# The first loads of a one-core decoder step, dealt out anew to three DMA queues, with the lower bounds moved into the first chunk

## The chip, the cores and the metric

One Trainium2 chip, of which the program uses one core. The metric is the device time of one execution in microseconds (us); below, "a run" is one timed execution. Lower is better.

## The reference, cut to what matters

One inference step of a hybrid decoder layer (width 2048) for 256 prompt tokens and 8 sample tokens. Only the start of the layer matters here: a modulation vector worked out from the condition `c`, a normalised and modulated `x`, and the input projection of it.

```python
mod = jax.nn.silu(c) @ p['w_ada'][l] + p['b_ada'][l]
sh1, sc1, gt1, sh2, sc2, gt2 = jnp.split(mod[:, None, :], 6, axis=-1)
h = rmsnorm(x, p['g_pre_mix'][l]) * (1.0 + sc1) + sh1
z = h @ p['w_in'][l]
...
p = jax.nn.softmax(hg_lb.astype(jnp.float32), axis=0)
return jnp.maximum(jnp.cumsum(p, axis=0) - p[0:1], 0.0)
```

The last two lines are the lower bounds of one of three recurrent branches. They depend on one small input, `hg_lb` (1024 numbers), and are needed when that branch is worked out, after the first part of the input projection. After the mixer follow an output projection and a squared-ReLU MLP, all in float32 built from pairs of rounded halves.

## The kernel before, in words

**The work.** Every large product is done as three products of rounded halves: a weight block `raw` is loaded, ScalarE rounds it (`whi`, L667), VectorE takes what is left (`wlo`, L671), and TensorE multiplies `whi` and `wlo` with the halves of the activations (`mm`, issued through the helper at L89). The weights run through one long list of blocks (`Stream`, L629), in the order in which TensorE uses them.

**The start.** The input projection begins in "chunks" of K (`CHUNKS`, L36): chunk 0 multiplies the first two 128-wide slices of `h`, chunk 1 the next two, chunks 2 to 4 four each. So the first products need only two slices of `h`, hence only the 2 x 256 columns of `w_ada` that give shift and scale for these slices. Those are loaded by class `First` (L518): for chunk 0 there are 8 batches `b` of two DMAs each, every DMA 128 x 2 x 256 numbers (256 KB), 16 DMAs in all. One batch makes 8 products on TensorE (`ada`, through L89; the trace counts two for each).

What must happen ahead of the first `mm` product:

- `cst` (an identity matrix `ident` and ones, 128 KB) and the conditions `c_prompt` and `c_sample` are loaded, transposed by TensorE (L200, L201), and ScalarE takes their SiLU into `cT` (L204, L205), which every `ada` product uses.
- `b_ada`, `g_pre_mix` and `g_post_mix` go to the tile `st1` by ScalarE's queue (L189 to L191), eight small vectors to the tile `st2` by GpSimd's queue (L196). `small_vectors()` (L208) transposes both on TensorE (L93) and VectorE copies the result to `vec` (L212).
- The four quarters of `x` (512 KB each) are loaded by SyncE's queue (L186). ScalarE squares and sums each (L294); VectorE adds the sums (`ss`, L139), works out the reciprocal root in a chain of small instructions (L249 to L255) and leaves it in `rx` (L301); ScalarE and VectorE scale `x` by it (L317, L318); TensorE transposes the first four slices (L93, from L312).
- The 16 `ada` DMAs land, TensorE does the `ada` products: batches 0 to 3 ahead of the transposes of `x`, batches 4 to 7 behind them. Their sum is copied (`gt`, L349), transposed, and becomes shift and scale (`mod`, L139 from L554; `A1`, L560); then `modulate_first` (L489) makes the first halves of `h`.
- `lower_bounds()` (L224) runs in this stretch as well: an exponential (L228), a reciprocal, six small VectorE instructions, two logarithms (L235, L239) and two more.

**What sets the order.** TensorE's, SyncE's and GpSimd's instructions stand in the order of the program here; those of ScalarE and VectorE are placed by a scheduler until L869, and from L872 to L950 (the chunks) all five engines stand in program order. A DMA started from SyncE or ScalarE takes one of eight semaphores in turn (DMAHW0 to DMAHW7 in the listings), one from GpSimd takes one of eight others (DMASW0 to DMASW7): before a DMA is started, the one that had its semaphore must have landed. So of the SyncE and ScalarE DMAs together no more than eight are under way, and a DMA waits for the one eight places ahead of it in the program.

**The chunks.** In chunk 0 ten granules (index `gi`) of 24 products each follow each other. Between them ScalarE and VectorE round the next weights and copy each granule's two accumulators out (`evict`, L918 by ScalarE, L920 by VectorE); TensorE has two accumulators of each kind, so the next granule needs them free. Meanwhile GpSimd's queue loads the `ada` weights for chunk 1 (L532).

Of the kernel before, what the change touches and what calls it, by code (L numbers as in the profile page):

```python
# [10 lines left out]
AF = mybir.ActivationFunctionType  # L11
ALU = mybir.AluOpType
# [3 lines left out]
P = 128  # L16
D = 2048
KT = D // P
# [17 lines left out]
CHUNKS = (2, 2, 4, 4, 4)  # L36
# [33 lines left out]
def hybrid_step_kernel(  # L70
# [8 lines left out]
    nc = tc.nc  # L79
    V, S = nc.vector, nc.scalar  # L80
# [48 lines left out]
    def tmp(shape, tag, bufs=2):  # L129
        return tp.tile(shape, F32, tag=tag, name=nm(tag), bufs=bufs)  # L130

    def const(shape, name, dt=F32):
        return cp.tile(shape, dt, tag=name, name=name)

    def mul(o, a, b):
        V.tensor_tensor(o, a, b, op=ALU.mult)  # L136

    def add(o, a, b):
        V.tensor_tensor(o, a, b, op=ALU.add)  # L139

    def sub(o, a, b):
        V.tensor_tensor(o, a, b, op=ALU.subtract)  # L142
# [21 lines left out]


    cst = const([P, 904], "cst")
    nc.sync.dma_start(cst[:, 0:256], consts[:, 0:256])
# [5 lines left out]
    def flat128(v):  # L173
        return v.rearrange("l (k p) -> (l k) p", p=P)
# [3 lines left out]
    nc.scalar.dma_start(st_c[0:KT, :], c_prompt.rearrange("b (k p) -> (b k) p", p=P))  # L178
    nc.scalar.dma_start(st_s, c_sample.rearrange("b (k p) -> (b k) p", p=P))

    xt = [[blk([P, 1024]) for _ in range(2)] for _ in range(2)]
    xsr = blk([P, P])
    nc.sync.dma_start(xsr, x_sample.rearrange("b o (k p) -> (b o k) p", p=P))
    for t in range(2):
        for hf in range(2):
            nc.sync.dma_start(xt[t][hf], x_prompt[0, t * P:(t + 1) * P, hf * 1024:(hf + 1) * 1024])  # L186
# [4 lines left out]
    nc.scalar.dma_start(st1[112:128, :], flat128(g_post_mix))  # L191
    st2 = blk([P, P])
    rows2 = [(g_pre_mlp, 16), (g_post_mlp, 16), (hg_lb, 8), (gla_b_up, 4), (hg_norm_g, 1), (gla_norm_g, 2), (sgu_ln_g, 8), (sgu_ln_b, 8)]
    n2 = 0
    for v, n in rows2:
        nc.gpsimd.dma_start(st2[n2:n2 + n, :], flat128(v))  # L196
        n2 += n

    ps = sm()
    T.transpose(ps[:, 0:KT], st_c[0:KT, :], ident[0:KT, 0:KT])  # L200
# [21 lines left out]
    lnlb, lnom, dlt, oml = (const([P, 8], n) for n in ("lnlb", "lnom", "dlt", "oml"))  # L222

    def lower_bounds():  # L224

        lt = [tmp([P, 8], f"lb{i}", 1) for i in range(4)]
        sub(lt[0], lbrawT, lbrawT)
        S.activation(lt[0], lt[0], AF.Exp)  # L228
        V.reciprocal(lt[1], lt[0])
        mul(lt[0], lt[0], lt[1])  # L230
        sub(lt[1], lt[0], lt[0])
        V.tensor_scalar(lt[1], lt[1], 0.0, None, ALU.max)
        V.tensor_scalar(lt[2], lt[1], 0.0, -1.0e30, ALU.is_equal, ALU.mult)
        V.tensor_scalar(lt[3], lt[1], 1.0e-19, None, ALU.max)
        S.activation(lnlb, lt[3], AF.Ln)  # L235
        add(lnlb, lnlb, lt[2])
        V.tensor_scalar(oml, lt[1], -1.0, 1.0, ALU.mult, ALU.add)
        V.tensor_scalar(lt[3], oml, 1.0e-19, None, ALU.max)
        S.activation(lnom, lt[3], AF.Ln)  # L239
        sub(dlt, lnom, lnlb)  # L240


# [275 lines left out]
    class First:  # L518
# [5 lines left out]
            self.w, self.at = {}, {}  # L524

        def load(self, b):
            queue = nc.gpsimd if self.k0 else nc.sync
            w = blk([P, self.kn, 2, self.n * P])
            w1 = w_ada[0, :, 0:2 * D].rearrange("k (r c) -> k r c", r=2)
            for i in range(self.kn):  # L530
                k = b * self.kn + i
                queue.dma_start(w[:, i], w1[k * P:(k + 1) * P, :, self.k0 * P:(self.k0 + self.n) * P])  # L532
            self.w[b] = w.rearrange("p k r c -> p k (r c)")
            self.at[b] = step[0]

# [93 lines left out]
    class Stream:  # L629
# [167 lines left out]
    def new_acc():  # L797
        return pmm.tile([P, 2, 512], F32, tag="mm", name=nm("mm"))
# [55 lines left out]
    stream[0].half_at = gap_at[0]  # L854
    first = First(0, CHUNKS[0])
    for b in range(8):
        first.load(b)
    for i in (0, 1, 2):
        stream[0].load(i)
    small_vectors()  # L860
    lower_bounds()
    for b in range(4):
        first.steps(b)
    scale_rows(xt, rx)
# [29 lines left out]
    for ci, n in enumerate(CHUNKS):  # L894
# [2 lines left out]
            to_load += [(at, parts[-1], b) for b, at in enumerate(LOAD_AT[ci])]  # L897
        k0 += n
    k0 = 0
    for ci, n in enumerate(CHUNKS):  # L900
        final = ci == len(CHUNKS) - 1
        gn = 4 // n
        ng = len(begin) // gn
        if not final:
            nxt = parts[ci].paced()
        for gi in range(ng):
            if ci or gi:
                accs = [new_acc() for _ in range(gn)]
            todo = begin[gi * gn:gi * gn + gn]

            def evict(acc):

                c0, dst, fn = todo.pop(0)
                z = acc[:, :, 0:NT]
                if ci:
                    add(dst, dst, z)
                elif todo:
                    S.copy(dst, z)  # L918
                else:
                    V.tensor_copy(dst, z)  # L920
                if final and fn is not None:
                    S.activation(dst, dst, fn)

            def between():

                step[0] += 1
                if not final:
                    next(nxt, None)

            load_due()  # L930
            if ci or gi:
                granule(win, 0, n, begin[gi * gn][0], gn * CW, accs, hH, hL, k0, True, True, evict, between)
# [653 lines left out]
    for m in range(8):  # L1586
        if m in PRE_AT:
            n = N_PRE // len(PRE_AT)
# [341 lines left out]
```

## Time and profile before

| | |
|---|---|
| time, median of 3 runs (lowest to highest) | 1794.4 us (1793.9 to 1795.85) |
| span of the profiled execution, first to last instruction | 1792.8 us |
| TensorE busy with products | 1770.3 us (99%) |
| TensorE busy with weight loads | 1686.2 us (94%) |
| VectorE busy | 1183.8 us (66%) |
| ScalarE busy | 1002.5 us (56%) |
| GpSimd busy | 140.5 us (8%) |
| moved by DMA | 442 MB, mean 247 GB/s |
| granted TensorE clock | 1.00 |

The profile has no time of its own for the profiled execution but the span. The median of the runs is 1.6 us longer than that span.

How to read it: rows of the timeline give start and duration in us, the engine, the line of the kernel, the operation, "out<-in" by the names of the tiles (their numbers left out), the count, and in brackets the idle time ahead of it with what ended that. PE is TensorE, PEld its weight loads, DVE VectorE, ACT ScalarE, POOL GpSimd, SP SyncE; a "q" behind an engine is its own instruction queue, which starts DMAs. Rows of the DMA view give the queue, the count, the size of each and the median time from the start of the issue to landing.

### The profile page before, as it was taken

The numbers are of one execution on the slowest core, as the hardware profiler recorded it, in microseconds if no ns is written. First come the engines' busy times: TensorE is split into PE (matmuls) and PEld (weight loads), VectorE is DVE, ScalarE is ACT, GpSimd is POOL, SyncE is SP. The second block draws the span as 40 slices with busy tenths as digits, with TensorE's granted clock in tenths as the row PEclk, the third lists the DMA queues.
The fourth block names the chain that finished last, engine by engine and source line by source line (L and its number), as shares of the span: only waits on it lengthen the run. The fifth ranks groups of instructions, "written<-read, shape, count | busy, mean of one in ns | idle before, by whom it ended". The sixth has DMA issues, their size and how long they took to land.

```text
span 1792.8 us, 42113 instructions
## 1 busy us (share of the span) xinstructions
PE 1770.3 (99%) x16970; PEld 1686.2 (94%) x16970; DVE 1183.8 (66%) x2079; ACT 1002.5 (56%) x1823; POOL 140.5 (8%) x228
## 2 busy tenths in 40 slices
PE   6999999999999999999999999999999999999998
PEld 5899999989999999899999989999999999999997
DVE  5676668697588697466566666645666666666666
ACT  5444554666766766655455665555454545454544
POOL 4222000101102012110000010000000000000000
PEclk9999999999999999999999999999999999999999
DMA  9998597789699789898866946776666666666663
GB/s 343 392 354 296 184 340 249 227 293 309 208 290 320 236 285 311 286 370 264 266 193 206 319 140 220 239 254 204 193 196 198 194 197 195 194 199 192 198 191 117
DMA packets 330179, 442.05 MB, mean 247 GB/s; under 512 B 14946, under 2 KB 276944, under 8 KB 329984
## 3 DMA queue, kind: packets, MB, share of 16 engines
q1 hardware_dynamic: 312160, 381.05, 65.5%
q0 software_dynamic: 17184, 57.85, 9.2%
q8 instruction: 133, 2.18, 0.5%
q14 instruction: 62, 0.51, 0.1%
q10 hardware_dynamic: 640, 0.47, 0.1%
HBM read 427.60 MB, written 11.70 MB: 245 GB/s over the span
## 4 chain that ended last, share of the span: by engine, by line
PE 95%; DMA 2%; DVE 2%; ACT 1%; issue 0%; SPq 0%; DVEq 0%; ACTq 0%
PE mm L89 86%; PE ada L89 5%; PE sm L89 3%; PE sm L93 1%; DMA b<-in_w_ada_dram 1%; DVE wlo L671 1%; DMA b<-in_x_prompt_dram 0%; DVE b L139 0%; DVE b L1670 0%; DVE b L142 0%; ACT b L1356 0%; ACT b L145 0%; SPq L532 0%; SPq L186 0%; DVE b L136 0%
## 5 line engine op out<-in xcount | busy, mean ns | idle before, releaser
L89 PE MATMUL mm<-b,whi 128*128 128x264 f32 x9248 | 1578.8, 277 | 1.3 <-DVE b L920 0.4
L89 PEld LDWEIGHTS mm<-b,whi 128*128 128x128 f32 x9248 | 1394.4, 189 | 35.0 <-issue 19.9
L89 PE MATMUL mm<-b,wlo 128*128 128x264 f32 x4624 | 1275.5, 276 | 0.0
L671 DVE TENSOR_TENSOR wlo<-raw,whi 128x512 fp32r<-128x512 f32 x1118 | 760.3, 690 | 462.1 <-ACT whi L667 459.2
L667 ACT CAST whi<-raw 128x512 fp32r<-128x512 f32 x1118 | 681.7, 617 | 620.2 <-DVE wlo L671 315.6
L89 PEld LDWEIGHTS mm<-b,wlo 128*128 128x128 f32 x4624 | 873.5, 189 | 0.2
L139 DVE TENSOR_TENSOR b<-b,mm 128x528 f32<-128x528 f32 (+1 forms) x137 | 95.7, 699 | 55.6 <-PE mm L89 49.0
L89 PE MATMUL ada<-b,cT 128*32 128x256 f32 (+2 forms) x888 | 66.2, 421 | 3.4 <-DMA b<-in_w_ada_dram 3.1
L89 PEld LDWEIGHTS ada<-b,cT 128*32 128x32 f32 x888 | 26.1, 112 | 34.1 <-issue 17.2
L1860 POOL TENSOR_TENSOR gs<-b,G 128x16 f32<-128x16 f32 x1 | 0.2, 222 | 714.1 <-DVE b L139 714.1
L532 POOL DMA_DIRECT2D b<-in_w_ada_dram x64 | 46.3, 726 | 44.1 <-PE ada L89 35.1
L1214 POOL DMA_DIRECT2D out_dram<-st x32 | 23.5, 735 | 234.0 <-DVE st L1213 227.6
L667 ACT CAST whi<-araw 128x512 fp32r<-128x512 f32 x38 | 23.1, 618 | 26.2 <-PE mm L89 22.0
L89 PE MATMUL ada<-araw,cT 128*32 128x512 f32 x264 | 35.6, 599 | 0.0
L1211 ACT ACTIVATE st<-st,fs 128x128 f32<-128x128 f32 (+1 forms) x96 | 35.2, 426 | 0.0
L136 DVE TENSOR_TENSOR b<-b,b 128x512 f32<-128x512 f32 (+1 forms) x47 | 34.4, 747 | 1.2 <-ACT b L1325 0.8
L1213 DVE SCALAR_TENSOR_TENSOR st<-vbc,b,st 128x128 f32<-128x128 f32 (+1 forms) x96 | 32.4, 392 | 1.2 <-ACT st L1211 1.2
L93 PE MATMUL sm<-cst,b 128*128 128x128 f32 (+1 forms) x149 | 21.5, 285 | 8.2 <-DMA b<-in_g_post_mix_dram 5.0
L671 DVE TENSOR_TENSOR wlo<-araw,whi 128x512 fp32r<-128x512 f32 x38 | 24.6, 686 | 5.3 <-ACT whi L667 5.3
L93 PEld LDWEIGHTS sm<-cst,b 128*128 128x128 f32 (+1 forms) x149 | 17.5, 147 | 9.2 <-issue 6.0
L142 DVE TENSOR_TENSOR b<-b 128x1024 f32<-128x1024 f32 (+1 forms) x24 | 24.4, 1022 | 1.5 <-PE ada L89 1.4
L142 DVE TENSOR_TENSOR b<-gt,b 128x528 fp32r<-128x528 f32 x32 | 22.7, 709 | 3.6 <-ACT whi L667 0.5
(303 smaller groups left out, 819.5 us busy)
## 6 DMA issues: line engine op xcount, KB each, us to landing
raw<-in_w_in_dram SPq DMA_DIRECT2D x225, 512.0 KB, 5.2
raw<-in_w_mlp_down_dram SPq DMA_DIRECT2D x128, 512.0 KB, 3.6
raw<-in_w_mlp_up_dram SPq DMA_DIRECT2D x125, 512.0 KB, 3.9
araw<-in_w_ada_dram SPq DMA_DIRECT2D x66, 512.0 KB, 6.1
b<-in_w_ada_dram SPq DMA_DIRECT2D x62, 512.0 KB, 6.8
b<-in_w_ada_dram POOLq DMA_DIRECT2D x48, 512.0 KB, 9.6
raw<-in_w_branch_dram SPq DMA_DIRECT2D x48, 512.0 KB, 4.7
raw<-in_w_out_dram SPq DMA_DIRECT2D x32, 512.0 KB, 4.5
```

Of the source, the lines that this page charges most:

```text
L89: return nc.tensor.matmul(out, w, x, **kw)
L93: return nc.tensor.transpose(*a)
L136: V.tensor_tensor(o, a, b, op=ALU.mult)
L139: V.tensor_tensor(o, a, b, op=ALU.add)
L142: V.tensor_tensor(o, a, b, op=ALU.subtract)
L532: queue.dma_start(w[:, i], w1[k * P:(k + 1) * P, :, self.k0 * P:(self.k0 + self.n) * P])
L667: self.last = [S.copy(hi, raw).ins, None]
L671: self.last[1] = V.tensor_tensor(lo, raw, hi.bitcast(F32), op=ALU.subtract).ins
L1211: S.activation(st[:, i, :], st[:, i, :], AF.Copy, scale=fs[:, h0 + i, b:b + 1])
L1213: V.scalar_tensor_tensor(st[:, i, :], v[:, i, :], k[:, h0 + i, NP + b:NP + b + 1], st[:, i, :], ALU.mult, ALU.add)
L1214: nc.gpsimd.dma_start(G.s_out(b, h0, nh), st)
L1860: Q.tensor_tensor(gs[:, 14:16, :], dst[:, :, NP:NT], G2[:, 14:16, 1:NC], op=ALU.mult)
```

## The change

- `x` is the first thing that SyncE's queue loads. `cst` and `x_sample` ahead of it go to ScalarE's queue, behind `c_prompt` and `c_sample`.
- The 16 `ada` DMAs for chunk 0 are issued by a new helper, `load_first`: even batches by SyncE's queue (8 DMAs), odd batches by GpSimd's (8 DMAs, behind its eight small loads). Their tiles are taken earlier, and `First` only takes them over.
- `lower_bounds()` becomes a generator of four parts. It runs in chunk 0, one part each after granules 5, 6, 7 and 8: the exponential; eight VectorE instructions; the two logarithms together; the last two VectorE instructions. A third temporary is reused so that both logarithms can follow each other.

```diff
-    nc.sync.dma_start(cst[:, 0:256], consts[:, 0:256])
...
     nc.scalar.dma_start(st_c[0:KT, :], c_prompt.rearrange("b (k p) -> (b k) p", p=P))
     nc.scalar.dma_start(st_s, c_sample.rearrange("b (k p) -> (b k) p", p=P))
 
+    nc.scalar.dma_start(cst[:, 0:256], consts[:, 0:256])
     xt = [[blk([P, 1024]) for _ in range(2)] for _ in range(2)]
     xsr = blk([P, P])
-    nc.sync.dma_start(xsr, x_sample.rearrange("b o (k p) -> (b o k) p", p=P))
+    nc.scalar.dma_start(xsr, x_sample.rearrange("b o (k p) -> (b o k) p", p=P))
...
+    w_first = [blk([P, 2, 2, CHUNKS[0] * P]) for _ in range(KT // 2)]
+
+    def load_first(queue, b):
+
+        for i in range(2):
+            k = 2 * b + i
+            src = w_ada[0, k * P:(k + 1) * P, 0:2 * D].rearrange("p (r c) -> p r c", r=2)
+            queue.dma_start(w_first[b][:, i], src[:, :, 0:CHUNKS[0] * P])
+
+    at2 = 0
     for v, n in rows2:
-        nc.gpsimd.dma_start(st2[n2:n2 + n, :], flat128(v))
-        n2 += n
+        nc.gpsimd.dma_start(st2[at2:at2 + n, :], flat128(v))
+        at2 += n
+    for b in range(KT // 2):
+        load_first(nc.gpsimd if b % 2 else nc.sync, b)
...
         S.activation(lt[0], lt[0], AF.Exp)
+        yield
         V.reciprocal(lt[1], lt[0])
...
         V.tensor_scalar(lt[3], lt[1], 1.0e-19, None, ALU.max)
+        V.tensor_scalar(oml, lt[1], -1.0, 1.0, ALU.mult, ALU.add)
+        V.tensor_scalar(lt[0], oml, 1.0e-19, None, ALU.max)
+        yield
         S.activation(lnlb, lt[3], AF.Ln)
+        S.activation(lnom, lt[0], AF.Ln)
+        yield
         add(lnlb, lnlb, lt[2])
-        V.tensor_scalar(oml, lt[1], -1.0, 1.0, ALU.mult, ALU.add)
-        V.tensor_scalar(lt[3], oml, 1.0e-19, None, ALU.max)
-        S.activation(lnom, lt[3], AF.Ln)
         sub(dlt, lnom, lnlb)
...
     for b in range(8):
-        first.load(b)
+        first.w[b] = w_first[b].rearrange("p k r c -> p k (r c)")
...
     small_vectors()
-    lower_bounds()
...
+    bounds = lower_bounds()
...
             if ci == 0 and 2 * gi + 8 < KT:
                 x_transposed(2 * gi + 8)
+            elif ci == 0 and gi >= 5:
+                next(bounds, None)
```

Two places show how instructions move.

ScalarE, the first rows of the program before (`b_86`, `b_87` are the tiles of the conditions, `b_100` is `st1`, `sm_113` the transposed conditions):

```order
L178 DMA b_86<-in_c_prompt_dram 16x128
L179 DMA b_87<-in_c_sample_dram 128x128
L204 ACT_TABLE_LOAD [waits DVE_49]
L204 ACTIVATE cT<-sm_113 128x16 [waits PE_49]
L205 ACTIVATE cT<-sm_113 128x16x8
L189 DMA b_100<-in_b_ada_dram 96x128 [waits DMAHW0_49]
L190 DMA b_100<-in_g_pre_mix_dram 16x128 [waits DMAHW1_49]
L191 DMA b_100<-in_g_post_mix_dram 16x128 [waits DMAHW2_49]
```

The same place on ScalarE now (`b_94` is the tile of `x_sample`, `b_90` the first quarter of `x`, `sm_137` the transposed conditions):

```order
L177 DMA b_85<-in_c_prompt_dram 16x128
L178 DMA b_86<-in_c_sample_dram 128x128
L180 DMA cst<-in_consts_dram 128x256
L183 DMA b_94<-in_x_sample_dram 128x128
L216 ACT_TABLE_LOAD [waits DVE_49]
L216 ACTIVATE cT<-sm_137 128x16 [waits PE_49]
L217 ACTIVATE cT<-sm_137 128x16x8
L189 DMA b_100<-in_b_ada_dram 96x128 [waits DMAHW0_49]
L190 DMA b_100<-in_g_pre_mix_dram 16x128 [waits DMAHW1_49]
L191 DMA b_100<-in_g_post_mix_dram 16x128 [waits DMAHW2_49]
L309 ACTIVATE b_160,ss_22_158<-b_90 128x1024 [waits DMAHW4_49]
```

Two DMAs have come in ahead; the three loads of `st1` still stand behind the SiLU of the conditions, and the squares of `x` behind these.

VectorE, where the sums of squares meet the small vectors, before (`ss` the sums of squares, `vec` the transposed small vectors from `sm_211`, `rr` the reciprocal root):

```order
L303 COPY xx_127<-sm_147 128x8
L139 TENSOR_TENSOR ss_14_134<-ss_14_134 128x2 [waits Activation_49]
L212 COPY vec<-sm_211 128x191 [waits PE_49]
L249 TENSOR_SCALAR sx_150<-ss_14_134 128x2 [waits DVE_49]
L302 COPY xx_127<-ss_14_134 128x2
L213 TENSOR_SCALAR vec<-vec 128x3 [waits DVE_49]
L251 TENSOR_SCALAR rr_15_135<-sx_150 128x10 [waits DVE_49]
L142 TENSOR_TENSOR lb_43_216<-vec 128x8
```

The same place on VectorE now:

```order
L318 COPY xx_151<-sm_171 128x8
L224 COPY vec<-sm_211 128x191 [waits PE_49]
L225 TENSOR_SCALAR vec<-vec 128x3 [waits DVE_49]
L139 TENSOR_TENSOR ss_22_158<-ss_22_158 128x2 [waits Activation_49]
L264 TENSOR_SCALAR sx_174<-ss_22_158 128x2 [waits DVE_49]
L317 COPY xx_151<-ss_22_158 128x2
L266 TENSOR_SCALAR rr_23_159<-sx_174 128x10 [waits DVE_49]
L136 TENSOR_TENSOR sa_175<-rr_23_159 128x10 [waits DVE_49]
```

Both instructions on `vec` now stand ahead of the sum `ss`, and the first instruction of the lower bounds is gone from here.

More of the change, by code (lines that the diff above doesn't have):

```diff
@@ L193, in hybrid_step_kernel @@
     rows2 = [(g_pre_mlp, 16), (g_post_mlp, 16), (hg_lb, 8), (gla_b_up, 4), (hg_norm_g, 1), (gla_norm_g, 2), (sgu_ln_g, 8), (sgu_ln_b, 8)]
-    n2 = 0
+    n2 = sum(n for _, n in rows2)
+    w_first = [blk([P, 2, 2, CHUNKS[0] * P]) for _ in range(KT // 2)]
[5 more added lines that the diff above has]
+    at2 = 0
     for v, n in rows2:
-        nc.gpsimd.dma_start(st2[n2:n2 + n, :], flat128(v))
-        n2 += n
+        nc.gpsimd.dma_start(st2[at2:at2 + n, :], flat128(v))
+        at2 += n
+    for b in range(KT // 2):
+        load_first(nc.gpsimd if b % 2 else nc.sync, b)
     ps = sm()
@@ L526, in load @@
         def load(self, b):
-            queue = nc.gpsimd if self.k0 else nc.sync
             w = blk([P, self.kn, 2, self.n * P])
@@ L531, in load @@
                 k = b * self.kn + i
-                queue.dma_start(w[:, i], w1[k * P:(k + 1) * P, :, self.k0 * P:(self.k0 + self.n) * P])
+                nc.gpsimd.dma_start(w[:, i], w1[k * P:(k + 1) * P, :, self.k0 * P:(self.k0 + self.n) * P])
             self.w[b] = w.rearrange("p k r c -> p k (r c)")
```

## Prediction

> **What bounds the kernel now.** The page first: how busy each engine is, and the chain that ended last.
>
> ```profile
> span 1792.8 us, 42113 instructions
> PE 1770.3 (99%) x16970; PEld 1686.2 (94%) x16970; DVE 1183.8 (66%) x2079; ACT 1002.5 (56%) x1823; POOL 140.5 (8%) x228
> PE 95%; DMA 2%; DVE 2%; ACT 1%; issue 0%; SPq 0%; DVEq 0%; ACTq 0%
> ```
>
> TensorE bounds it: 99% busy, 95% of the chain. The 22.5 us in which it does nothing (1792.8 - 1770.3) are all this change can touch. Where they lie, the table of stages tells (stretch, its length, then busy us of PE, PEld, DVE, ACT, POOL, granted clock, DMA share, GB/s):
>
> ```profile
> 0.00:10.00 10.00, 1.54 (x5) 0.97 (x5) 2.06 (x9) 3.95 (x7) 5.54 (x15) 1.00 0.76 244
> 10.00:20.00 10.00, 6.93 (x71) 3.12 (x72) 4.93 (x29) 7.54 (x11) 0.00 (x0) 1.00 0.97 314
> 20.00:30.00 10.00, 8.05 (x103) 6.01 (x102) 4.68 (x13) 4.84 (x11) 2.86 (x5) 1.00 1.06 398
> 30.00:40.00 10.00, 9.26 (x81) 8.83 (x80) 8.86 (x15) 7.02 (x14) 8.04 (x12) 1.00 1.03 389
> 40.00:50.00 10.00, 10.00 (x138) 9.68 (x137) 5.41 (x10) 5.34 (x9) 4.33 (x6) 1.00 1.04 402
> ```
>
> TensorE idles 8.5, 3.1, 1.9 and 0.7 us in the first four stretches, 14.2 in all, then not at all from 40 to 50. From 40 us on it is fed, so a microsecond won or lost ahead of the first `mm` product is, as long as nothing behind it runs dry, one at the end. What holds up that first product, the chain in order of time and the timeline say:
>
> ```profile
> 3.06 8.79 DMA b<-in_x_prompt_dram
> 18.28 6.57 DMA b<-in_w_ada_dram
> ...
> 24.90 0.42 PE L89 MATMUL ada<-b,cT 128*32 128x128 f32 x8 [1.37 <-DMA b<-in_w_ada_dram]
> 27.25 0.72 PE L89 MATMUL mm<-b,whi 128*128 128x264 f32 x4
> ```
>
> The first two rows are of the chain, the others of the timeline. The last quarter of `x` lands at 3.06 + 8.79 = 11.85. The last `ada` DMA starts at 18.28, since it has to wait for the one eight places ahead of it, and lands at 24.85; the first `mm` product follows 2.4 later, at 27.25. A second path meets it, by way of the root of `x`:
>
> ```profile
> 11.94 1.06 ACT L294 ACTIVATE b<-b 128x1024 f32<-128x1024 f32 x1 [0.41 <-DMA b<-in_x_prompt_dram]
> 13.12 0.16 DVE L139 TENSOR_TENSOR ss<-ss 128x2 f32<-128x2 f32 x1 [6.52 <-ACT b L294]
> 13.20 0.35 DVE L212 COPY vec<-sm 128x191 f32<-128x191 f32 x1
> 15.91 2.19 ACT L317 ACTIVATE b<-b,rx 128x1024 f32<-128x1024 f32 x2 [1.30 <-DVE rx L301]
> 18.89 1.97 PE L93 MATMUL sm<-cst,b 128*128 128x128 f32 x8
> 51.76 1.95 PE L89 MATMUL ada<-b,cT 128*32 128x128 f32 x64
> ```
>
> From `ss` (13.12) it takes 2.8 to `rx` (L317 starts at 15.91), 1.1 for half of L317 (the first half of `x` is enough for these transposes), 1.97 for the transposes, 1.95 for four batches of `ada` products whose weights lie ready (the row from chunk 1), and 1.9 from the end of those to the first `mm` (24.90 + 0.42 to 27.25). Together 9.7 us from `ss`: alone, this path would have given the first product at 22.8. So today the weights decide, with 4.4 us in hand on the other path.
>
> **The change part by part.** Loads first, by these rows (those ahead of the dots are of the timeline, the others of the DMA view):
>
> ```profile
> 0.74 0.39 SPq L167 DMA_DIRECT2D cst<-in_consts_dram  x1
> 1.19 0.44 ACTq L179 DMA_DIRECT2D b<-in_c_sample_dram  x1
> 1.65 1.85 SPq L186 DMA_DIRECT2D b<-in_x_prompt_dram  x4
> 3.12 1.00 PE L93 MATMUL sm<-cst,b 16*128 16x16 f32 x3 [3.12 <-DMA cst<-in_consts_dram]
> 5.17 0.53 ACTq L191 DMA_DIRECT2D b<-in_g_post_mix_dram  x1
> 5.46 0.50 POOL L196 DMA_DIRECT2D b<-in_sgu_ln_b_dram  x1
> 11.33 0.82 PE L93 MATMUL sm<-cst,b 128*128 128x128 f32 x2 [5.02 <-DMA b<-in_g_post_mix_dram]
> 45.59 0.72 POOL L532 DMA_DIRECT2D b<-in_w_ada_dram  x1 [0.35 <-issue]
> ...
> cst<-in_consts_dram SPq DMA_DIRECT2D x1, 128.0 KB, 2.2
> b<-in_b_ada_dram ACTq DMA_DIRECT2D x1, 48.0 KB, 6.5
> b<-in_w_ada_dram POOLq DMA_DIRECT2D x16, 256.0 KB, 8.0
> b<-in_w_ada_dram SPq DMA_DIRECT2D x16, 256.0 KB, 5.4
> b<-in_sgu_ln_b_dram POOLq DMA_DIRECT2D x1, 4.0 KB, 5.9
> ```
>
> *`x`* starts at 0.74 in place of 1.65: its last quarter lands some 0.9 sooner, near 10.9, and its last square is summed near 12.2.
>
> *The weights of `ada`.* SyncE issues eight, GpSimd eight. SyncE's wait on the DMAs eight places ahead: `x_sample`, the four quarters of `x`, then `b_ada`, `g_pre_mix` and `g_post_mix`. GpSimd's wait for its own small loads, the last of which has landed near 11.4 (issued at 5.46, plus 5.9), the others before it, and each takes 0.72 to issue; the last is out near 13. With 8.0 to landing, this queue's time in chunk 1, GpSimd's half is there at 21.0. SyncE's last goes out about 1 us behind the landing of `g_post_mix`; at the time taken below, 14.2, it lands at 14.2 + 1 + 5.4 = 20.6. So the weights free the first product at 21.0 + 2.4 = 23.4, 3.9 earlier than now.
>
> Against this stands a rule. In the table of stages the DMA share is 0.97 from 10 to 20 at only 314 GB/s, and 1.06 at 398 in the next stretch, so a full share doesn't mean full speed. The Trainium skill ("DMA: Bandwidth & Descriptors", section "Issuing engines are not separate DMA queues") says that DMAs from any engine end up on the same 16 DMA engines, and that several issuing engines save issue time alone. By that rule the weights would land earlier only by the 0.9 of `x`; the trace agrees as to the share, not as to the speed. That case is the third rival below.
>
> *`cst` and `x_sample`* pay. They were issued at 0.74 and 1.18 and met empty engines (2.2 to landing for `cst`). Now `cst` is third on ScalarE's queue, behind `c_sample`, at 1.19 + 0.44 = 1.6, beside 2 MB of `x`. Bounds: 2.2 as before, or 6.5 like `b_ada`, which was issued with all of `x` under way. I take the middle, 4.35, since about half of `x` is out by then: `cst` lands at 6.0 in place of 2.9. What is queued behind it: TensorE's transposes of the conditions, the SiLU on ScalarE, and in ScalarE's order `b_ada`, `g_pre_mix`, `g_post_mix` and the four squares. Before, `g_post_mix` landed (11.3) 8.2 after TensorE had `cst` (3.12). The same gives 6.0 + 8.2 = 14.2. The squares begin near 8.5 and, at 1.2 each (11.94 to `ss` at 13.12), end at 13.3: not last. `x_sample`, fourth on that queue, lands by 2.1 + 6.5 = 8.6 at the latest and is needed only for the root.
>
> *The order on VectorE.* `vec` now stands ahead of `ss`. So the root waits for TensorE's transposes of `st1` and `st2` (0.82) and the copy (0.35, and a little for the small product behind it): `ss` at 14.2 + 1.3 = 15.5 in place of 13.12. From there 9.7 less 0.15 for three foreign instructions that leave the stretch, 9.55: first product at 25.05. This is later than the 23.4 of the weights, so it decides. **Start: 27.25 - 25.05 = 2.2 us won**, half of what the weights alone would give.
>
> *The lower bounds.* Their instructions in the start lay beside the wait for weights; taking them out is worth no more than those 0.15. In chunk 0 they meet these rows of the timeline (the last one is of the chain, three granules of 24 products):
>
> ```profile
> 13.10 1.28 ACT L228 ACT_TABLE_LOAD   x1
> 14.40 0.21 ACT L228 ACTIVATE lb<-lb 128x8 f32<-128x8 f32 x1
> 50.52 0.60 ACT L918 COPY b<-mm 128x528 f32<-128x528 f32 x1 [0.84 <-PE mm L89]
> 56.65 0.71 DVE L920 COPY b<-mm 128x528 f32<-128x528 f32 x1 [0.76 <-PE mm L89]
> 58.11 0.60 ACT L918 COPY b<-mm 128x528 f32<-128x528 f32 x1 [0.96 <-PE mm L89]
> 61.42 0.59 ACT L918 COPY b<-mm 128x528 f32<-128x528 f32 x1
> 56.72 8.31 PE mm L89 x72
> ```
>
> The exponential with its table (1.28 + 0.21 = 1.5) falls into the 0.84 idle ahead of the copy at 50.52, which comes 0.65 later; TensorE then does the 1.95 of `ada` at 51.76, so this is covered. Without that cover it would cost the 0.65. The eight VectorE instructions (at 0.17, 1.4) meet 0.76 idle ahead of 56.65: 0.6 late, while that accumulator is wanted again only about half a granule (1.4) on. The logarithms with their table (1.28 + 2 x 0.21 = 1.7) meet 0.96 ahead of 58.11 and push all on ScalarE by 0.74. The copy at 61.42, which waits for nobody, ends at 62.75 then; TensorE wants that accumulator at 56.72 + 2/3 x 8.31 = 62.25. **Cost 0.5**, between 0 (if the casts ahead are done early) and 1.7 (if none of it is covered).
>
> The 0.02 between the table load (13.10 to 14.38) and the exponential (14.40) leaves no room for more. The Trainium skill ("ScalarE: Activation LUTs", section "What ACT_TABLE_LOAD costs") counts 2.66 us for each switch, 1.28 of load and 1.38 of draining; with that the logarithms would cost an estimated 1.9 in place of 0.5 and the time would be 1794.1; the trace agrees with the load alone.
>
> *Behind the start* nothing moves. GpSimd's loads for chunk 1 follow the first product, and SyncE's weights start earlier (10 DMAs fewer ahead of them), so the lead of the loads doesn't shrink. That TensorE has no slack there, the waits of TensorE from 27 us to the end show, eight kinds, of which the longest and the shortest:
>
> ```profile
> PE sm L89 <- DVE vsb L139: 0.6, 1, 0.6
> ...
> PE sm L89 <- ACT vt L1811: 0.2, 1, 0.2
> ```
>
> **The sum.** Span 1792.8 - 2.2 + 0.5 = 1791.1. The median of the runs lies 1.6 above the profiled span; with it 1792.7.
>
> **The rivals.** What a measurement of this kernel can tell from no change is about 0.2%, 3.6 us: below 1790.8 counts as faster, above 1798.0 as slower.
>
> *The small loads aren't held up* (chance 0.16). With 2.2, `cst` is there at 3.8, `g_post_mix` at 12.0, `ss` at 13.3, and that path gives 22.9. Then the weights decide, at 23.4: 3.85 won, 0 to 0.5 lost, 1790.5 to 1791.0. For it: `cst` is issued when only a part of `x` is. Against it: `x` gets the engines first.
>
> *The small loads become the bound, and the kernel slower* (0.14). Place: PE's transposes of `st1`, ahead of all `ada` products and of the root. Each microsecond of `g_post_mix` past 16.4 costs one; with the lower bounds' 0.5, past 15.9. With `cst` at 1.6 + 6.5 = 8.1 and 8.2 more it lands at 16.3: 0.4 slower, 1794.8. If the three loads wait longer still, since GpSimd's weights now come in between, like the last quarter of `x` (8.79 rather than 6.0), it is 19.1 and the first product 29.95: 2.7 + 0.5 slower, 1797.6. For it: 5.02 idle ahead of 11.33 today was due to these very loads. Against it: less lies ahead of them once `x` is in.
>
> *The 16 DMA engines bound the weights whatever the queue* (0.18). They land 0.9 earlier, the first product comes at 26.35, less 0.5: 1794.0. This is the case by the Trainium skill's rule on issuing engines, above. For it: the share of 0.97. Against it: the 314 GB/s beside 398 in the next stretch.
>
> **How the numbers follow.** My forecast, with `st1` as the bound but early enough, gets 0.52: 1792.7. The two remaining rivals of no change lie within 1794.0 and 1794.8. The range goes from the fast end of the first rival, less the 0.2 by which a median may differ, 1790.3, to the dear end of the lower bounds on the slow middle case (1794.8 + 1.2, and 0.6 towards the slowest one): 1796.6. Faster by over 0.2%: 0.11, most of it from the first rival at its 1790.5. Slower: 0.06, from the second past its dear end. Same: 0.83.
>
> **What would show it.** Right: `cst` lands between 4 and 8, not at 2.9; PE's two transposes of `st1` begin at 13 to 16; `ss` follows `vec`; no `ada` batch of 4 to 7 is waited for; the first `mm` comes near 25, and a gap of about half a microsecond lies at the end of chunk 0. Wrong: the transposes of `st1` at 12 or sooner (first rival), after 16.5 (second), or a wait for `ada` weights right ahead of the first product (third). If the first product comes earlier and the end doesn't follow, then a wait in the chunks has eaten it, and my reading of the stages fails.

## The result, and the profile after

The kernel became slower, by a little: 1796.77 us median (1794.37 to 1799.93, 21 runs) against 1794.44 (1792.14 to 1795.93, 21 runs of the kernel before beside them). The ratio is 1.0016, 95% interval 1.0010 to 1.0022, some 1.8 to 3.9 us; the two medians lie 2.3 apart. The forecast was 1792.7 with 1796.6 as the top of its range: the time lies above it, and on the other side of "before".

The page of the profiled execution (1796.27 us by its run), its head:

```profile
span 1794.5 us, 42126 instructions
PE 1769.6 (99%) x16970; PEld 1688.1 (94%) x16970; DVE 1183.6 (66%) x2079; ACT 1001.9 (56%) x1823; POOL 146.4 (8%) x236
```

TensorE does the same work (1769.6 for 1770.3) and idles 24.9 us in place of 22.5. The table of stages says where (length, then busy us of PE, PEld, DVE, ACT, POOL, granted clock, DMA share, GB/s):

```profile
10.00:20.00 10.00, 4.37 (x45) 2.38 (x45) 5.45 (x27) 5.76 (x10) 3.59 (x6) 1.00 0.96 323
20.00:30.00 10.00, 9.46 (x124) 7.75 (x122) 3.64 (x11) 4.62 (x9) 1.67 (x4) 1.00 1.04 387
60.00:70.00 10.00, 9.67 (x98) 8.34 (x97) 7.63 (x14) 5.94 (x11) 7.95 (x12) 1.00 0.95 342
```

From 10 to 20 us TensorE is busy 4.37 us, where it was 6.93; from 20 to 30 it catches some of that up (9.46 for 8.05). The DMA engines moved hardly more: 323 GB/s where it was 314. And there is a new gap of 0.33 between 60 and 70.

The chain of waits, in order of time (start, length, what), its first part:

```profile
2.14 7.73 DMA b<-in_x_sample_dram
9.89 0.38 SPq L202
...
11.34 9.17 DMA b<-in_w_ada_dram
20.56 1.51 PE ada L89 x24
```

SyncE's first load of `ada` starts at 9.89, when `x_sample` has landed: that load is eight places ahead of it among the DMAs of SyncE and ScalarE. SyncE's fourth, the second half of batch 2, takes 9.17 and lands at 20.51. Behind it TensorE has, in the order of the program, the rest of batches 2 and 3, the transposes of `x` and batches 4 to 7. The timeline shows the same place from TensorE and VectorE:

```profile
14.86 0.82 PE L93 MATMUL sm<-cst,b 128*128 128x128 f32 x2 [2.26 <-DMA b<-in_g_post_mix_dram]
16.19 0.15 DVE L139 TENSOR_TENSOR ss<-ss 128x2 f32<-128x2 f32 x1
18.83 2.19 ACT L332 ACTIVATE b<-b,rx 128x1024 f32<-128x1024 f32 x2 [3.55 <-DVE rx L316]
20.56 1.51 PE L89 MATMUL ada<-b,cT 128*32 128x128 f32 x24 [0.54 <-DMA b<-in_w_ada_dram]
22.00 1.97 PE L93 MATMUL sm<-cst,b 128*128 128x128 f32 x8
23.89 2.61 PE L89 MATMUL ada<-b,cT 128*32 128x128 f32 x64
27.07 1.04 PE L93 MATMUL sm<-cst,b 128*128 128x128 f32 x8
28.45 0.72 PE L89 MATMUL mm<-b,whi 128*128 128x264 f32 x4
```

The first `mm` comes at 28.45 in place of 27.25, 1.20 later. The first half of `x` was scaled at about 19.9 (L332 at 18.83, plus 1.1) and waited until 22.00 for TensorE. And no weights are waited for behind 20.56: the four last batches run through. The DMA view of the first 40 us has the times to landing:

```profile
b<-in_w_ada_dram SPq DMA_DIRECT2D x8, 256.0 KB, 8.8
cst<-in_consts_dram ACTq DMA_DIRECT2D x1, 128.0 KB, 6.8
b<-in_x_sample_dram ACTq DMA_DIRECT2D x1, 64.0 KB, 7.7
b<-in_g_post_mix_dram ACTq DMA_DIRECT2D x1, 8.0 KB, 4.6
```

The rest of the loss lies at the end of chunk 0. First ScalarE in the timeline, then TensorE's next product there:

```profile
58.36 1.28 ACT L251 ACT_TABLE_LOAD   x1
...
63.16 0.58 ACT L932 COPY b<-mm 128x528 f32<-128x528 f32 x1
...
63.80 0.49 PE L89 MATMUL mm<-b,whi 128*128 128x264 f32 x2 [0.33 <-ACT b L932]
```

The table load pushes ScalarE's copies back, and TensorE waits for the one at 63.16. The same two places in the chain, the first pair of rows before the change, the second after it:

```profile
53.72 2.90 PE mm L89 x24
65.03 1.86 PE ada L89 x32
...
54.84 2.90 PE mm L89 x24
66.76 1.86 PE ada L89 x32
```

By the chain, a granule in the middle of chunk 0 starts 1.12 later than before (54.84 for 53.72), the `ada` products behind this gap 1.73 later (66.76 for 65.03), and the span ends 1.7 later. So in these two executions 1.1 was lost in the start and 0.6 here, and nothing after. The medians lie 2.3 apart, 0.6 more than these 1.7; where the rest lies, two profiles can't tell.

### The profile page after: what moved, and what is told of

Its sections match the earlier page's. It is cut to its first block, busy times and chain, and to the rows that moved or that the text cites. A ratio compares the mean times of both kernels' runs of the same rounds, so it can differ in the third digit from the quotient of the medians.

```text
span 1794.5 us, 42126 instructions
## 1 busy us (share of the span) xinstructions
PE 1769.6 (99%) x16970; PEld 1688.1 (94%) x16970; DVE 1183.6 (66%) x2079; ACT 1001.9 (56%) x1823; POOL 146.4 (8%) x236
## 4 chain that ended last, share of the span: by engine, by line
PE 96%; DMA 1%; DVE 1%; ACT 1%; issue 0%; ACTq 0%; SPq 0%; DVEq 0%
PE mm L89 86%; PE ada L89 5%; PE sm L89 3%; PE sm L93 1%; DMA b<-in_w_ada_dram 1%; DMA b<-in_x_sample_dram 0%; DVE wlo L685 0%; DVE b L139 0%; DVE b L1686 0%; ACT whi L681 0%; ACT b L1372 0%; ACT b L145 0%; SPq L202 0%; DVE b L136 0%; ACT b L516 0%
## 5 line engine op out<-in xcount | busy, mean ns | idle before, releaser
L89 PEld LDWEIGHTS mm<-b,whi 128*128 128x128 f32 x9248 | 1394.4, 189 | 35.4 <-issue 19.9
L681 ACT CAST whi<-araw 128x512 fp32r<-128x512 f32 x38 | 23.1, 618 | 26.7 <-PE mm L89 23.6
L142 DVE TENSOR_TENSOR b<-b 128x1024 f32<-128x1024 f32 (+1 forms) x24 | 24.4, 1019 | 0.8 <-PE ada L89 0.7
```

The costliest lines, as they stand in the source:

```text
L89: return nc.tensor.matmul(out, w, x, **kw)
L681: self.last = [S.copy(hi, raw).ins, None]
```

## The experiments

Each kernel is timed against the kernel before on its own chip; times of different groups are compared by their ratios to it. "First product" is the first `mm` in the profiled execution. That execution lies up to 2.2 us off the median of its kernel, so it shows where time goes, and the median says how much.

**The parts undone.** First the lower bounds put back behind `small_vectors()`:

```diff
     small_vectors()
+    for _ in lower_bounds():
+        pass
...
-            elif ci == 0 and gi >= 5:
-                next(bounds, None)
```

> The change, but with the lower bounds worked out in the start again. Three theories on the late first product (28.45 us in the changed kernel, 27.25 before): S, x_sample on ScalarE's queue holds up SyncE's ada loads through the shared semaphore; C, the late constants delay st1 and with it the root of x; G, GpSimd's loads crowd SyncE's out of the DMA engines. All three expect the first product where the change has it, near 28.4, or up to 0.3 later. The lower bounds, apart from these, should give back the 0.61 us that the change loses in chunk 0: time 0.6 below the changed kernel, no wait of TensorE for ScalarE's copy at the end of chunk 0.

Measured: 1802.43 (5 runs), ratio 1.0050 (1.0037 to 1.0062). All theories missed this. ScalarE's timeline:

```profile
17.45 0.21 ACT L240 ACTIVATE lb<-lb 128x8 f32<-128x8 f32 x1 [5.48 <-DVE lb L142]
...
26.39 2.19 ACT L332 ACTIVATE b<-b,rx 128x1024 f32<-128x1024 f32 x2 [2.68 <-DVE rx L316]
```

The scheduler now puts the exponential ahead of the squares of `x`. It needs `vec`, which is late, so ScalarE stands still for 5.48 and `x` is scaled at 26.39, where it was 18.83. So with the loads of the new kernel, taking the lower bounds out of the start is worth much more than the 0.15 of the forecast: it keeps the late `vec` off ScalarE's path.

Then `x_sample` moved behind `x` in the program, still on ScalarE's queue, so that it is no longer eight places ahead of SyncE's first load:

```diff
-    nc.scalar.dma_start(xsr, ...)
     for t in range(2):
...
+    nc.scalar.dma_start(xsr, ...)
```

> The change, but with x_sample's load behind those of x in the program, so that SyncE's first ada load waits for the first quarter of x (landed near 6.5) and no longer for x_sample (landed at 9.87). ScalarE issues x_sample behind the SiLU then, so st1 may land 0.4 later. S: the first ada loads go out near 7 in place of 9.89, batch 2 lands 3 us earlier, first product near 26, time 2 to 2.5 below the changed kernel. C: first product no earlier than 28.4. G: no earlier than 28, since GpSimd's loads run as before.

Measured: 1797.87, ratio 1.0021 (1.0012 to 1.0030). The timeline of TensorE:

```profile
14.76 0.47 PE L93 MATMUL sm<-cst,b 128*128 128x128 f32 x1 [5.54 <-DMA b<-in_x_sample_dram]
17.61 0.81 PE L93 MATMUL sm<-cst,b 128*128 128x128 f32 x2 [0.19 <-DMA b<-in_g_post_mix_dram]
...
22.78 1.97 PE L93 MATMUL sm<-cst,b 128*128 128x128 f32 x8 [0.78 <-ACT b L332]
29.85 0.72 PE L89 MATMUL mm<-b,whi 128*128 128x264 f32 x4
```

SyncE's loads start at 8.44, and batches 0 to 3 wait for no weights any more. But `x_sample` now stands behind the SiLU on ScalarE, the three loads of `st1` behind it, and the transposes of `x` wait for the root. The first product comes at 29.85, where theory S foretold 26. The hold by `x_sample` is real, but with it gone the other path is longer still.

All 16 loads of `ada` on SyncE's queue:

```diff
-        load_first(nc.gpsimd if b % 2 else nc.sync, b)
+        load_first(nc.sync, b)
```

> The change, but with all 16 ada loads on SyncE's queue. G: each lands some 5.5 after its issue again in place of 6.6 to 9.4, batches 0 to 3 are there by 17 to 18, the last near 24, first product near 26.5, time 2 below the changed kernel. S and C: all 16 wait for x_sample, the last lands past 25.5, first product at 28 or later, time the same or higher.

Measured: 1796.23, ratio 1.0015 (1.0007 to 1.0024), the same as the changed kernel. Its chain of waits:

```profile
19.94 6.72 DMA b<-in_w_ada_dram
26.70 0.66 PE ada L89 x8
```

Without GpSimd's loads SyncE's take 5.9 to landing, but they start at 9.87, held by `x_sample` as in the changed kernel, and there are twice as many: the last lands at 26.66, 1.8 later than before, as theories S and C have it; theory G foretold 24. With two queues the last landed 3.2 sooner, near 23.4, and the time is the same: by the two chains, what the deal won on the last load was lost on batch 2.

The constants and `x_sample` on SyncE's queue ahead of `x`, as before the change; the rest as in the changed kernel:

```diff
+    nc.sync.dma_start(cst[:, 0:256], consts[:, 0:256])
...
-    nc.scalar.dma_start(cst[:, 0:256], consts[:, 0:256])
-    nc.scalar.dma_start(xsr, ...)
+    nc.sync.dma_start(xsr, ...)
```

> The change, but with cst and x_sample on SyncE's queue ahead of x again (x 0.9 later); the halves of the ada loads on two queues and the lower bounds in chunk 0 stay. S and C: SyncE's first ada load goes out near 3.5, st1 lands near 11.5 to 12, first product at 23 to 24, time 4 to 5 below the changed kernel, 2 to 3 below the kernel before. G: SyncE's ada loads still take 7 to 9 to land beside GpSimd's, first product at 26 to 27.5, time within 1 of the kernel before.

Measured: 1793.98, ratio 1.0001 (0.9992 to 1.0010): level with before. A row of its chain, and its timeline:

```profile
9.87 9.67 DMA b<-in_w_ada_dram
```

```profile
12.83 0.82 PE L93 MATMUL sm<-cst,b 128*128 128x128 f32 x2 [6.54 <-DMA b<-in_g_post_mix_dram]
19.58 1.51 PE L89 MATMUL ada<-b,cT 128*32 128x128 f32 x24 [2.29 <-DMA b<-in_w_ada_dram]
27.52 0.72 PE L89 MATMUL mm<-b,whi 128*128 128x264 f32 x4
```

`st1` is transposed 2.0 sooner than in the changed kernel, and that wins nothing at once: batch 2, still late, is waited for. The first product comes 0.9 sooner, at 27.52: theory G foretold 26 to 27.5, S and C 23 to 24. By this pair the late small loads are what made the changed kernel slower than before (a second pair follows below); without them the other two parts still give no gain.

The lower bounds in chunk 0 alone (the kernel above with all `ada` loads on SyncE's queue):

> The kernel before with the third part of the change alone: the lower bounds in chunk 0, all loads in the places they had before (the 16 loads of ada on SyncE's queue, the constants and x_sample ahead of x on it). All theories: the first mm product near 27.2, as before, a gap of about half a microsecond for TensorE at the end of chunk 0, and 0.3 to 0.7 slower than before. If the lower bounds in the start cost something that the profile of before hides, it is not slower.

Measured: 1794.65, ratio 1.0002 (0.9993 to 1.0011). TensorE's first product behind the gap:

```profile
63.10 0.49 PE L89 MATMUL mm<-b,whi 128*128 128x264 f32 x2 [0.34 <-ACT b L932]
```

The gap is there again. The median lies 0.9 above before, which 11 runs cannot tell from none; the place and the wait are shown, the 0.6 is read from the profiles. This kernel and the one with all loads on SyncE's queue and late small loads (1.0015) differ by the place of the small loads alone: that is the second pair. The first product stands at 28.46 here, not near 27.2 as foretold; more on this under TensorE's speed.

**How many loads, and which.** GpSimd's queue takes batches 6 and 7 only, with the small loads ahead of `x`:

```diff
-        load_first(nc.gpsimd if b % 2 else nc.sync, b)
+        load_first(nc.gpsimd if b >= 6 else nc.sync, b)
```

> Constants and x_sample on SyncE's queue ahead of x, the lower bounds in chunk 0, and GpSimd's queue takes only the last four loads of ada (batches 6 and 7), SyncE's the other twelve. Theory G (eight loads on GpSimd's queue starve SyncE's, and batch 2, which comes late, has the transposes and four batches behind it): GpSimd's four land near 16, SyncE's take about 5.5 to landing, the last near 22; no load is waited for ahead of the transposes of x later than about 18.5; first mm 24 to 25, and the time 1791 to 1792, below before. Rival, the 16 DMA engines set when 4 MB of ada weights are in, whoever issues them: SyncE's last lands near 24, first mm 26 to 26.5, 1793.5.

Measured: 1794.41, ratio 1.0001 (0.9992 to 1.0010); of the 11 runs one took 6552.91 and is left out of the ratio. In its profile the first product stands at 25.57, 2.9 ahead of the changed kernel and some 2 us ahead of the even deal with the small loads early. That is between theory G's 24 to 25 and its rival's 26 to 26.5. The median shows no gain on before, so theory G's 1791 to 1792 failed. The chain:

```profile
12.59 6.88 DMA b<-in_w_ada_dram
19.52 0.66 PE ada L89 x8
```

What bounds it is still a load of batches 0 to 3 with transposes and four batches behind it. The same deal of the loads in the changed kernel, with the small loads late:

> The kernel after with GpSimd's queue taking only batches 6 and 7; the constants and x_sample stay on ScalarE's queue. Theory C (late constants delay st1, the root and the transposes of x): st1 transposed near 14.9, ss 16.2, first mm 25.7 to 26, 1794.2. Theory S (x_sample's late landing holds SyncE's loads to 9.9, whatever GpSimd does): SyncE's twelve loads end near 25, first mm near 27.4, 1795.7. Against the run with the constants first it tells what the late small loads cost where GpSimd takes little.

Measured: 1795.20, ratio 1.0007 (0.9998 to 1.0016); first product 27.82, 2.2 later than with the small loads early. Its time is nearer to theory S than to theory C, and its path is a hold of the same kind by another small load: `g_post_mix`, the first of these rows of the chain, landed at 15.52. SyncE's eighth load, the second half of batch 3, stands eight places behind it, starts only then, and TensorE does that half batch at 21.02.

```profile
10.17 5.35 DMA b<-in_g_post_mix_dram
15.54 5.44 DMA b<-in_w_ada_dram
```

Batches 0 to 3 on GpSimd's queue and 4 to 7 on SyncE's, all else as in the changed kernel (`b < 4` in the same line):

> The kernel after with GpSimd's queue taking batches 0 to 3 and SyncE's batches 4 to 7. The same loads by the same queues, only dealt out otherwise. Theory G (SyncE's late loads hurt because batch 2, ahead of the transposes of x and of four batches, is among them): batches 0 to 3 end near 20.8, transposes to 22.8, SyncE's last lands near 24.1 and is waited for right ahead of the first mm, which comes at 26 to 26.5: 1794.5, 2 below after. If the root is what bounds it, the first mm stays near 28.4 and the time at 1796.8.

Measured: 1796.17, ratio 1.0014 (1.0005 to 1.0023). The first product stays at 28.26. Theory G foretold 26 to 26.5 and failed:

```profile
16.12 0.82 PE L93 MATMUL sm<-cst,b 128*128 128x128 f32 x2 [3.38 <-DMA b<-in_g_post_mix_dram]
21.14 0.66 PE L89 MATMUL ada<-b,cT 128*32 128x128 f32 x8 [0.26 <-DMA b<-in_w_ada_dram]
21.73 1.97 PE L93 MATMUL sm<-cst,b 128*128 128x128 f32 x8
23.63 2.69 PE L89 MATMUL ada<-b,cT 128*32 128x128 f32 x64
```

Now it is GpSimd's last load that ends batch 3 late (8.37 to landing), `st1` is late by another 1.3, and from the transposes to the first product it is 6.5 us without a wait for a load. So giving the needed loads to the other queue did not help. Whether that is due to the late batch 3 or to the late `st1` this run can't tell: scaled `x` was there near 21.2 (L332 at 20.09, plus 1.1), just ahead of batch 3's last products. And the last 64 products take 2.69, where the row of chunk 1 had 1.95 for as many.

**TensorE's speed.** That last row was the lead. In the changed kernel 24 `ada` products take 1.51 (63 ns each) at 20.56, 64 take 2.61 (41) at 23.89 and, in chunk 1, 1.95 (30); eight transposes take 1.97 at 22.00 and 1.04 at 27.07. The granted clock in the table of stages is 1.00 throughout, but for the start that is no reading. The trace's own list of clock periods begins only at 25.3 us in the changed kernel (at 20.9 before), with full clock, and the view counts what lies ahead of the list as full. Where a slow period of the start is on record, in the run with all loads on SyncE's queue, the column (the last but two) shows it, and eight transposes at 28.09 take 1.91 there:

```profile
23.30:26.60 3.30, 1.57 (x47) 0.85 (x36) 0.00 (x0) 0.00 (x0) 0.00 (x0) 1.00 1.06 394
26.70:30.00 3.30, 3.30 (x20) 2.92 (x21) 1.56 (x6) 1.95 (x5) 0.61 (x2) 0.50 1.05 407
```

The profile of the lower bounds alone has such a period too, from 25.8 to 29.2, with which its late first product fits. So TensorE works at half speed in the changed kernel until about 25 us. To test it, products of constants (`ident` with `cst`, into an accumulator that is not used yet) fill TensorE's waits in the changed kernel:

```diff
+    warm(256)
+    warm(256)
     small_vectors()
+    warm(256)
     for b in range(4):
+        if b == 2:
+            warm(256)
-        first.steps(b)
+        first.steps(b, lambda: warm(P) if b == 2 else None)
```

> The kernel after with five products of constants added for TensorE to do while it waits (two ahead of the transposes of st1, one behind them, one ahead of batch 2, a half one within it); loads and all else stay. Theory H (TensorE runs at half speed until it has been busy for some 4.5 us: in the profile of after the ada products take 61 ns each until about 25 us and 30 ns then, and a transpose 246 against 130 ns, with the granted clock at 1.00 throughout): the 24 products behind the late load take 0.8 in place of 1.5, the transposes of x 1.04 in place of 1.97, the last 64 products 1.95 in place of 2.6; first mm product at 26 to 26.8, and 1794.5 to 1795.2, about 2 below after. Rival (the products are slow because the DMAs load the memory, or the waits lie elsewhere): those rows stay as they are, first mm at 28.4 or up to 1 later, 1796.8 to 1797.8.

Measured: 1795.14, ratio 1.0006 (0.9997 to 1.0015). TensorE's timeline:

```profile
19.43 1.22 PE L89 MATMUL mm<-cst 128*128 128x256 f32 x2
21.65 0.86 PE L89 MATMUL ada<-b,cT 128*32 128x128 f32 x24
22.44 1.09 PE L93 MATMUL sm<-cst,b 128*128 128x128 f32 x8
23.46 1.95 PE L89 MATMUL ada<-b,cT 128*32 128x128 f32 x64
27.34 0.72 PE L89 MATMUL mm<-b,whi 128*128 128x264 f32 x4
```

The same 24 products, transposes and 64 products take 0.86, 1.09 and 1.95: 2.2 less, close to what was foretold for each, with the same loads. Of this 1.1 is given back, since the added products at half speed stood ahead of batch 2, whose rest began at 21.65 in place of 20.56. The first product comes 1.1 sooner, at 27.34 and not at the 26 to 26.8 of the forecast; the median's ratio lies lower than that of the changed kernel, with intervals that overlap. The Trainium skill ("TensorE: Matmul & The Clock Gate", Part 1, "What's actually happening") says that the array runs at 1.2 in place of 2.4 GHz until it has been busy for at least one window of some 3.4 us. The factor of two is that of the rows, and the time here was longer than one such window. In the changed kernel some 21 of the 64 products must still have been slow (21 x 63 + 43 x 30 ns = 2.61), which puts the step near 25.2, 4.6 behind 20.56, where the unbroken work began. That agrees with the 25.3 at which the trace's list of clock periods begins.

**Towards a better one.** Small loads ahead of `x`, GpSimd on batches 4 and 5, the transposes of `x` behind batch 2:

```diff
+        load_first(nc.gpsimd if b in (4, 5) else nc.sync, b)
...
-    for b in range(4):
+    for b in range(3):
...
-    for b in range(4, 8):
+    for b in range(3, 8):
```

> Constants and x_sample ahead of x, the lower bounds in chunk 0; GpSimd's queue takes batches 4 and 5 only, and TensorE does the transposes of x behind batch 2 in place of batch 3. Against the run in which GpSimd took batches 6 and 7 (first mm 25.57). Theory W (what is late is what lies on TensorE behind the last load that it waits for, not the loads alone): transposes of x at 17.5 to 18.5, SyncE's last load near 22 to 23, first mm 24 to 25, 1792 to 1793. If the loads set it whatever the order, the first mm stays at 25.5, 1793.5 to 1794.4.

Measured: 1793.67, ratio 0.9997 (0.9988 to 1.0006); first product 26.00, no load waited for behind 17.25:

```profile
17.25 1.87 PE L89 MATMUL ada<-b,cT 128*32 128x128 f32 x24 [0.59 <-DMA b<-in_w_ada_dram]
19.05 1.97 PE L93 MATMUL sm<-cst,b 128*128 128x128 f32 x8
20.95 3.09 PE L89 MATMUL ada<-b,cT 128*32 128x128 f32 x80
```

The time is that of the rival (1793.5 to 1794.4); the first product was neither theory's number. The second half of batch 1 came late, and the path from there was TensorE's own work, more than half of it at half speed. With the products of constants as well:

> The run with GpSimd on batches 4 and 5 and the transposes behind batch 2, and the same five products of constants. Theory H: no product at half speed from about 17 on; where SyncE's last load is waited for, the first mm follows 2.4 behind it, at 24 to 24.7, 0 to 0.5 below the run without; a result above that run by 0.5 to 1 speaks for products that stand in the way. The best of the versions if H and W both hold: 1792.

Measured: 1794.83, ratio 1.0001 (0.9992 to 1.0010), first product 26.51. The transposes took 1.09, the 80 products 2.39, 1.6 less together, but the constants' products stood in the way by 1.9 (18.10 to 19.25, and 19.84 to 20.57). The forecast of 24 to 24.7 failed; it had named this as the reason if the run came out behind the one without. Last, the kernel two above with the lower bounds moved on to chunk 1:

```diff
-            elif ci == 0 and gi >= 5:
+            elif ci == 1 and gi >= 2:
```

> The run with GpSimd on batches 4 and 5 and the transposes of x behind batch 2, with the four parts of the lower bounds moved on from chunk 0 to chunk 1 (behind its granules 2 to 5), where ScalarE idles 3.5 us ahead of its pairs of rounding casts. If the gap at the end of chunk 0 is the logarithms' table load meeting ScalarE's copies (theory B): no wait of TensorE for a copy at 61 to 63, 0.6 below the same kernel with the bounds in chunk 0, 0.9990 to 0.9995 of the kernel before, 1793.1 by its time of 1793.67. If any place in the chunks costs as much, the gap comes back near 75 and the time stays.

Measured: 1793.57, ratio 0.9998 (0.9988 to 1.0007). The chain through the end of chunk 0 is unbroken, three granules without a wait:

```profile
53.77 8.32 PE mm L89 x72
```

So theory B holds for the place of the gap, while the gain of 0.6 is below what 11 runs tell. This version and the one with the lower bounds in chunk 0 lie below the changed kernel (their intervals end below the start of its own); neither is told from the kernel before.

## Why the prediction was wrong

**What was right.** `vec` stands ahead of `ss` and the small loads are late; the lower bounds cost 0.6 (0.5 forecast) at the end of chunk 0; nothing behind it moves; GpSimd's half of the weights was there at about 20 (21.0 forecast); the last of all weights landed at about 23.4 (SyncE's last issue at 14.74, with 8.7 to landing), 1.4 sooner than before; no batch of 4 to 7 was waited for. Of its signs two failed, `cst` between 4 and 8 (it landed near 8.5) and the first product near 25.

**The step that failed** is "So the weights free the first product at 21.0 + 2.4 = 23.4", and with it the verdict that `st1` decides. Two things in it were wrong. SyncE's half was given its old 5.4 to landing; it took 8.8. The likely reason is that two queues' loads are under way together while the total hardly rose (314 to 323 GB/s from 10 to 20 us). The weights as a whole land only 1.4 sooner, near the 0.9 of the third rival. This agrees with the rule that the forecast named there (the Trainium skill, "DMA: Bandwidth & Descriptors", section "Issuing engines are not separate DMA queues"). And 2.4 is the way from the *last* batch to the first product. Which load would be waited for was not asked: it is SyncE's fourth, in batch 2, at 20.51, and from there it was 7.9 us to the first product. The third rival's price of 1794.0 failed for the same reason.

**The sum, step by step.** The path over the root was forecast at 25.05 and came at 28.45, 3.4 later. `ss` came at 16.19 for 15.5: 0.7. `cst` took 6.8 to landing, more than the 6.5 that was the dear bound, and landed 2.5 later than the 6.0 taken; the loads behind it on ScalarE's queue were quicker than taken, so that `g_post_mix` was only 0.7 late. From scaled `x` (19.9) to the transposes (22.0) 2.1 were lost to batch 2. The last four batches took 2.61, not 1.95: 0.7. That row came from chunk 1, where TensorE has long been at full speed; before the change the last batches of the start ran at full speed too: 40 products from 21.61 on took 1.30 (32 ns).

**Which part of the change.** The late small loads are shown to cost the difference to before: with them first again the ratio goes from 1.0016 to 1.0001, with intervals that only touch. With all loads on SyncE's queue it goes from 1.0015 to 1.0002, with batches 6 and 7 on GpSimd's from 1.0007 to 1.0001; there the intervals overlap, but all three pairs lie the same way. They act twice, through `st1` and through the hold on SyncE's first load; undoing the hold alone, by `x_sample` later on the same queue, won nothing (1.0021), as the other way became longer. The forecast called `x_sample` "needed only for the root" though it listed it among the DMAs that SyncE's loads wait for. The second rival had the right sign and the right loads, with `st1` as its place; in the changed kernel's profile it is only one of the two. Its condition did not come true: `g_post_mix` landed near 14.7, ahead of the 15.9 from which it was to cost time. So that the measured time lies within its prices (1794.8 to 1797.6) is luck.

**What stays open.** How the 1.2 us divides between the late load and half speed is shown for one execution only. Why the split in two queues brings no gain in the median even where the profile shows the first product 2 us sooner (batches 6 and 7 on GpSimd's queue) was not settled: the times of 11 runs there spread over more than 2 us, and one profile is one of them (the 6552.91 aside). TensorE's speed may have a part in it: among the profiles of the runs level with before, the list of clock periods begins anywhere from 19.8 to 24.4 us. No run tests that.

## What to carry to other kernels

Price a load that moves by what the engine still has to do behind the batch that it belongs to, not by the last one. Giving half of the loads to a second queue starts them sooner, but here they shared what the DMA engines moved, which hardly rose; look for the load that is needed first and see that it does not come last. Before a small load is moved off the head of a queue, list all that waits for it: its users, what stands behind its users on their engines, and the DMAs that wait for its semaphore.

## What the runs showed of the hardware

- TensorE at half speed after waits: 63 against 30 ns for an `ada` product, 246 against 130 for a transpose, until some 4.6 us of unbroken work in the changed kernel; products of constants bring it up. The time is not a fixed one: from the last wait for a load to the begin of the clock list it was 3.3 in the kernel before (17.60 to 20.9) and 5.2 with the transposes behind batch 2 (17.25 to 22.4).
- Full speed was lost again without a long pause: with all loads on SyncE's queue TensorE was busy 1.57 of the 3.3 us from 23.3 to 26.6, with no wait above 1.6, and the granted clock was 0.50 from 26.7 to 30.0.
- The view of the granted clock reads 1.00 where the trace has no clock period on record, as in the slow start here.
- A small load issued 0.9 us later and on ScalarE's queue, beside 2 MB of `x`, took 6.8 us to landing in place of 2.2 (`cst`), and 7.7 in place of 2.0 (`x_sample`).
- With eight loads on each of two queues, those of SyncE took 8.8 in the changed kernel and 9.0 with the small loads early (5.4 to 5.9 when alone), while the GB/s of the changed kernel's stage stayed within 3%. It was not so in every case: with `x_sample` later SyncE's were issued over 9.5 us in place of 6.1, and took 5.7.
